# Placing the operands of 512-column products, and an earlier copy of x, in a four-layer float32 trunk

## The chip, the core and the metric

The kernel runs on one core of a Trainium2 chip. The metric is the time of one execution on the device in microseconds (us), the median of several. A profile is one further execution, recorded instruction by instruction. Engines: PE (TensorE: products), DVE (VectorE), ACT (ScalarE), POOL (GpSimd) and SP (SyncE); the last two mainly issue DMAs here.

## The reference

512 rows of 1,024 columns, all in float32, go through four layers. Each layer adds a mixer's output to x and then a gated FFN's; a root-mean-square norm precedes both, and one ends the trunk.

```python
for layer in range(DEPTH):            # 4
    h = rmsnorm(x, norm_mix[layer])
    mix = (s5_mixer, gla_mixer, diff_attn_mixer)[layer % 3](h, ...)
    x = x + mix
    h = rmsnorm(x, norm_ffn[layer])
    g, u = split(h @ w_gate_up, 2)    # 1024 x 5632
    x = x + (silu(g) * u) @ w_down    # 2816 x 1024
return rmsnorm(x, norm_final)
```

Layers 0 and 3 have the S5 mixer (a diagonal state space scan, a GELU and a gated product with `w_glu`, 1024 x 2048), layer 1 gated linear attention, layer 2 differential attention (eight heads, each of two softmaxes).

## The kernel before

**Products.** A float32 operand is kept as two float32r parts, a high part (ACT casts, L334) and a low part (DVE subtracts, L338). A product is three PE instructions: high x high, high x low, low x high (`mm3`, L351 to L353). The first operand of `matmul` after the output is held in the array in pieces of 128 columns; the second streams through it, 512 columns at a time. In `gemm_b` (down products, GLU, output products) the weights' parts `whl` stream and the activations are held: `act` in the FFNs, `zT` after S5, `oT` after the attentions, `hT` for the projections. In `gemm_a` (the first FFN's gate and up products, L351 to L353 with the tile name `any`) the weights are held and `hT` streams. The scores of differential attention (L1916) hold `qs` and stream `ks`.

**The fast FFN.** FFNs 1 to 3 use a Strassen-like scheme with seven products of quarters, 256 columns wide (L566). `seven_block` makes one block of 256 hidden columns: `one` to `seven` are the products, `*_out` take results out of PSUM, `gate1` and `four_out` apply SiLU, `add` sums weight quarters. The streamed sides are quarters of x and sums of them: "11" and "12" (tile `sides`) and "1", "2", "4", "3", "22" (tiles `side`). `left.total`, `high` and `low` form them. Weight quarters are loaded by SP; sums of two are formed by a second DMA on POOL that accumulates (L602, argument `plus`). The eleven blocks go in groups of 4, 4 and 3, each followed by a down product over 512-column halves.

**Order around the change.** Between the calls of `hand_all` and `hand` the order of every engine is that of the program text; elsewhere only PE's is (in the attentions), or a scheduler orders by priority and dependence. The string `plan` in `ffn` writes out the head of an FFN, blocks 0 ("a") and 1 ("b") interleaved. `ahead` stages weights of the first blocks while the mixer's last product still runs; at the second one it calls `total("3")`, two DVE subtractions (L199).

**The copy of x.** Layer 3's S5 wants the rows in another order. So the third FFN (`turn=True`) sends x to DRAM and back (`turn_x`, L804 and L806, each 2 MB, issued by POOL), and the row factors r with it. It is called at block 2, after that block's last accumulating DMA. POOL is in order: it waits at L806 until L804 has landed.

**Places in SBUF.** Tiles of a pool lie one behind the other, pools of a layer begin where the long-lived pools end. Adding up their sizes: the tiles of `hp` (hT, halves, sides) and `wp` (whl, wst) start at 192 modulo 256 bytes; the small pool (`self.sp`) has eight rooms of 32 bytes for each of its names and ends at 132,992, which is 128 modulo 256. So the layers' tiles (act, oT, side, slot, hl, qs) start at 128. zT is in a pool at the right end of SBUF, at 224.

**Heads of attention.** `prepare(j)` (L1885) splits a head's q and k into `hl` (one room), and eight small POOL DMAs rearrange it into `qs` and `ks`; `ks` lies in a weights' room (`wp`, name whl, five rooms).

**Norms with a power.** `normed` (L442) is used for the opening norm and the last one: Square on ACT (L450), an add on DVE (L437), a power on POOL (L439), then the scaling. `ms` holds the sums.

Of the kernel before, what the change touches and what calls it, by code (L numbers as in the profile page):

```python
# [11 lines left out]
F32 = mybir.dt.float32  # L12
# [4 lines left out]
ALU = mybir.AluOpType  # L17
# [128 lines left out]
class Sides(Left):  # L146
# [18 lines left out]
    def ahead(self, n):  # L165

        w = [self.tr.staged(self.quarter(0, 0, b), 4, 256) for b in range(len(self.heads), len(self.heads) + n)]
        self.heads += [self.tr.halves(y, 4, 256) for y in w]
        if len(self.heads) == 2:
            self.total("3")  # L170

    def open(self, pool, names):

# [89 lines left out]
class Trunk:  # L263
    def __init__(self, ctx, tc, ins, out):
        self.ctx, self.tc, self.nc = ctx, tc, tc.nc
        self.i = ins
        self.out = out
        self.rot = 0
# [12 lines left out]
        self.two_pi = float(np.nextafter(np.float32(TWO_PI), np.float32(0)))  # L281
        self.mhalf = self.cp.tile([P, 8], F32, name="mhalf")
        nc.vector.memset(self.mhalf[:], -0.5)
        self.ones = self.cp.tile([P, P], F32, name="ones")
        nc.gpsimd.memset(self.ones[:], 1.0)
        self.dq = nc.sync
        self.jobs = iter(())
        self.pend = []
        self.guard, self.lazy = None, False

    def hand_all(self):
        E = mybir.EngineType
# [149 lines left out]
    def normed(self, xt, g, out, pool, aside=False):  # L442

        nc = self.nc
        if pool is None:
            junk = self.wp.tile([P, D], F32, tag="wst", name="sq", bufs=3)
        else:
            junk = pool.tile([P, D], F32, tag="sq", name="sq", bufs=2)
        ms = self.sp.tile([P, 1], F32, tag="ms", name="ms")
        nc.scalar.activation(junk[:], xt, AF.Square, scale=1.0 / 32.0, accum_out=ms[:])  # L450
        r = self.rsqrt(ms[:], 1, 1e-6)
        if out is None:
            h = pool.tile([P, D], F32, tag="h", name="h", bufs=2)
            nc.vector.scalar_tensor_tensor(h[:], xt, r[:], g[:], op0=ALU.mult, op1=ALU.mult)
            return h
        if aside:
            nc.scalar.mul(junk[:], xt, r[:])
            gr = lambda y: y.rearrange("p (g c) -> p g c", c=16)
            nc.gpsimd.tensor_tensor(out, gr(junk[:]), gr(g[:]), op=ALU.mult)
# [45 lines left out]
    def ffn_plain(self, l, left, after=None, aside=None):  # L505
# [2 lines left out]
        wgu, wd = i["ffn_w_gate_up"][l], i["ffn_w_down"][l]  # L508
        nxt = None
        with self.tc.tile_pool(name=f"ffn{l}", bufs=1, reuse_waits="tile") as fp:  # L510
            self.jobs = aside(fp) if aside else iter(())
            first = True
            j0 = 0
# [57 lines left out]
    def seven_block(self, fp, slots, left, wgu, b, turn):  # L571
# [20 lines left out]
        def load(name, q, half, plus=None, room=None):  # L592
            if name in ("11", "3"):
                W[name] = self.staged(left.quarter(q, half, b), 4, 256)
            else:
                W[name] = slots.pop(0) if room is None else room
                if room is not None:
                    lent.add(name)
                nc.sync.dma_start(W[name][:], left.quarter(q, half, b))
            w = W[name]  # L600
            if plus:
                self.added = nc.gpsimd.dma_start(w[:], left.quarter(*plus, b), accum_op=ALU.add)  # L602

        def done(name):
            if name not in lent:
# [106 lines left out]
    def ffn(self, l, left, after=None, turn=False, aside=None):  # L712
# [5 lines left out]
        with self.tc.tile_pool(name=f"ffn{l}", bufs=1, reuse_waits="tile") as fp:  # L718

            room = lambda: fp.tile([P, 2, 4, 256], F32, tag="act", name="lent", bufs=4)  # L720
            left.open(fp, ("1", "2", "4", "3", "22") if l < 3 else ("1", "2"))
            if l == 3:
                lent = room()
            slots = [fp.tile([P, 4, 256], F32, name=f"slot{n}") for n in range(SLOTS)]
# [4 lines left out]
            blocks = [self.seven_block(fp, slots, left, wgu, b, turn) for b in range(FFN_HIDDEN // 256)]  # L729
            f = blocks[:2]  # L730
            if l == 3:
                left.open(fp, ("4", "3", "22"))
            for w, n, *room in (
                ("room21", 0), ("room1", 0, lent[:, 0]), ("room21", 1), ("room1", 1, lent[:, 1]), ("room22", 0),
# [1 line left out]
            ):  # L736
                f[n][w](*room)

            plan = """
                split21a one:a split21b square flush one:b total1 one_out:a finish high1 low1 total2 split1a high2 low2  # L740
                one_out:b two:a two:b split1b high3 two_out:a five:a add22a highSa two_out:b lowSa five_out:a five:b
                add22b highSb diag lowSb low3 split3a six:a spread five_out:b rows six:b six_out:a split3b seven:a
                six_out:b total4 split22a high4 low4 seven:b seven_out:a split22b three:a seven_out:b gate1:a gate1:b
                high22 low22 three:b add21a highFa add21b lowFa highFb lowFb four:a four:b three_out:a three_out:b
            """
            for step in plan.split():
                name, _, n = step.partition(":")
                if n:
# [5 lines left out]
                elif name in ("finish", "diag", "spread", "rows"):  # L754
                    getattr(left, name)()
                elif name == "square":
                    left.square(NT - 1, 1)
                elif name == "flush":
                    self.flush()
                else:  # L760
                    word = next(w for w in ("total", "high", "low") if name.startswith(w))
                    getattr(left, word)(name[len(word) :])
# [5 lines left out]
            for nb in (4, 4, 3):  # L768
                acts = []
                for n in range(b0, b0 + nb):  # L770
                    b = blocks[n]
                    if n > 1:
                        for w in ("direct", "room1", "room22", "room21", "summed"):
                            b[w]()
                    if turn and n == 2:

                        with self.tc.issue_after(self.added.ins):
                            r = self.turn_x(left.r)
                    if n > 1:
                        for step in ("one", "one_out", "five", "five_out"):  # L780
                            b[step]()
# [599 lines left out]
    def s5_first(self, ctx):  # L1381
        nc, i = self.nc, self.i
        xin = self.xp.tile([P, NT, D], F32, tag="x", name="xin")
        zpool = ctx.enter_context(self.tc.tile_pool(name="zT0", bufs=1, side="right"))
        zT = zpool.tile([P, 2, KT, SEQ], F32R, name="zT")
        with self.tc.tile_pool(name="s5_0", bufs=1) as p:
            scr, more = (self.hp.tile([P, 4096], F32, tag="hT", name=f"scr{z}") for z in range(2))
            oms = [more[:, 1024 * z : 1024 * z + 1024].rearrange("p (a b) -> p a b", a=2) for z in range(2)]
# [73 lines left out]
    def s5_second(self, l, ctx, left):  # L1462
        nc = self.nc
        zpool = ctx.enter_context(self.tc.tile_pool(name="zT1", bufs=1, side="right"))
        zT = zpool.tile([P, 2, KT, SEQ], F32R, name="zT")
        with self.tc.tile_pool(name="s5_1", bufs=1) as p:
            room = p.tile([P, 6, 512], F32, name="room2")
            parts = (("in", 0, 2, 2), ("cs", 2, 5, 3), ("out", 5, 8, 2))
# [26 lines left out]
    def s5_glu(self, L, zT, accs, after):  # L1495
# [5 lines left out]
        with self.tc.tile_pool(name=f"s5g_{L}", bufs=1) as p:  # L1501
            for d in range(2):
# [15 lines left out]
                        evac_b(t, accs[t])  # L1518
                else:
                    self.gemm_b(stat, wg, KT, D + d * 512, evac_b)  # L1520
                ahead = (lambda: nxt.ahead(2)) if L and d else None
                self.gemm_b(stat, wg, KT, d * 512, evac_a, tail=4 if d else 0, ahead=ahead)
        return nxt

# [1 line left out]
    def gla(self, l, left, after):  # L1526
# [3 lines left out]
        wo = i["gla_w_o"][0]  # L1530
        self.hand(mybir.EngineType.PE)
        with self.tc.tile_pool(name="gla", bufs=1) as p:
            big = lambda name, tag="g8", bufs=5: p.tile([P, 4, 512], F32, tag=tag, name=name, bufs=bufs)
            late = lambda name: big(name, "g8late", 3)
            oT = [p.tile([P, 2, 4, SEQ], F32R, name="oT0"), None]
# [195 lines left out]
            for d in range(2):  # L1731
                self.gemm_b(
                    so, wo, KT, d * 512, self.add_x(d, nxt), tail=4 if d else 0, between=() if d else late,
                    ahead=(lambda: nxt.ahead(2)) if d else None,
                )
        return nxt

# [52 lines left out]
    def diff(self, l, left, after):  # L1790
# [2 lines left out]
        w, wo = i["diff_w_qkv"][0], i["diff_w_o"][0]  # L1793
        self.hand(mybir.EngineType.PE)
        with self.tc.tile_pool(name="diff", bufs=1) as p:
            T = lambda tag, bufs=2: p.tile([P, 512], F32, tag=tag, name=tag, bufs=bufs)
            oT = [p.tile([P, 2, 4, SEQ], F32R, name="oT0"), None]
            qks = [p.tile([P, 2, 4, SEQ], F32, tag="qk", name="qk", bufs=2) for _ in range(2)]
# [86 lines left out]
            def prepare(j):  # L1885


                hl = p.tile([P, 2, 2, SEQ], F32R, tag="hl", name="hl")
                src = qks[j // 4][:, :, j % 4]
                nc.scalar.copy(hl[:, 0], src)  # L1890
                v.tensor_tensor(hl[:, 1], src, hl[:, 0].bitcast(F32), op=ALU.subtract)
# [64 lines left out]

            def normalised(j):
                st, o_s = kept.pop(j)
                q2 = self.sp.tile([P, NT], F32, tag="q2", name="q2")
                v.tensor_tensor(q2[:], st[:, 0], st[:, 0], op=ALU.mult)  # L1960
                v.scalar_tensor_tensor(q2[:], q2[:], 1e-5, st[:, 1], op0=ALU.mult, op1=ALU.add)
                rs = self.rsqrt(q2[:], NT, 0.0)
# [175 lines left out]
```

## Time and profile before

| | |
|---|---|
| median of 3 runs | 2391.58 us (2383.74, 2391.58, 2391.62) |
| profiled execution | 2382.31 us, its span 2380.6 us |
| granted PE clock | 0.982 of full speed, mean |
| ACT, DVE busy | 1073.0 us (45%), 1487.1 us (62%) |
| HBM read, written | 275.92 MB, 23.99 MB |

The span runs from the first to the last instruction. A row of the timeline has its start, its duration, the engine, the line, the operation, output and inputs, shapes, and in brackets the idle time before it with what ended it. The duration of a PE instruction is its latency; the next starts earlier, so the rate is the distance between starts. PEld is the loading of the held operand, which overlaps PE.

### The profile page before, as it was taken

To read this page: it belongs to the slowest core of one execution; us is meant where nothing else is said; L and a number is where in the kernel's file an instruction comes from. 1 tells how busy PE (TensorE), PEld (TensorE's weight loads), DVE (VectorE), ACT (ScalarE), POOL (GpSimd) and SP (SyncE) were. 2 spreads that over 40 slices of the span, in tenths; PEclk is the share of its full clock that TensorE was granted. 3 is DMA by queue.
4 is the path that set the end of the run, shared out by engine and by line. 5 is a ranking of instruction groups with operands and counts; after the bars stand their busy time and mean duration, and the time that the engine had idled before them with its cause. 6 is when DMAs were issued, how large, how long until landed. Compare 5 with 4: busy or idle time off the path is not lost. (4 is left out here: it accounts for less than half of the span.)

```text
span 2380.6 us, 35208 instructions
## 1 busy us (share of the span) xinstructions
PE 2269.0 (95%) x14055; PEld 1962.8 (82%) x14055; DVE 1487.1 (62%) x2311; ACT 1073.0 (45%) x1749; POOL 266.8 (11%) x335
## 2 busy tenths in 40 slices
PE   4799999999999999999999998989999899999997
PEld 3578888788877789898987887888989788999996
DVE  7774565555443459585753666875847874967674
ACT  4463445444352346252544665653635233634442
POOL 3330100111000011010001221110000000101000
PEclk9699999999999999999999999999999899999999
DMA  4123344544332258564345465694732645666521
GB/s 110 34 52 138 95 138 143 166 129 166 118 103 85 71 143 208 137 177 124 111 142 117 107 133 145 170 243 115 195 98 89 214 158 150 170 179 154 162 76 67
DMA packets 275502, 317.42 MB, mean 133 GB/s; under 512 B 45653, under 2 KB 214377, under 8 KB 274058
## 3 DMA queue, kind: packets, MB, share of 16 engines
q1 hardware_dynamic: 227210, 238.14, 31.9%
q0 software_dynamic: 48128, 77.02, 15.7%
q8 instruction: 111, 1.82, 0.3%
q14 instruction: 53, 0.43, 0.1%
HBM read 275.92 MB, written 23.99 MB: 126 GB/s over the span
## 5 line engine op out<-in xcount | busy, mean ns | idle before, releaser
L338 DVE TENSOR_TENSOR whl<-wst,whl 128x1024 fp32r<-128x1024 f32 x294 | 359.0, 1223 | 363.1 <-ACT whl L334 362.3
L334 ACT CAST whl<-wst 128x1024 fp32r<-128x1024 f32 x294 | 308.4, 1050 | 530.5 <-PE acc L353 354.8
L566 PE MATMUL a<-side,whl 128*128 128x256 f32 x2376 | 291.2, 279 | 14.2 <-ACT r L638 6.0
L566 PEld LDWEIGHTS a<-side,whl 128*128 128x128 f32 x2376 | 281.4, 190 | 16.2 <-ACT whl L334 6.9
L351 PE MATMUL acc<-whl,act 128*128 128x512 f32 x704 | 276.5, 393 | 0.7 <-DVE g L611 0.7
L353 PE MATMUL acc<-whl,act 128*128 128x512 f32 x704 | 276.9, 393 | 0.0
L352 PE MATMUL acc<-whl,act 128*128 128x512 f32 x704 | 275.6, 391 | 0.0
L566 PE MATMUL c<-side,whl 128*128 128x256 f32 x1584 | 192.4, 278 | 3.6 <-DVE whl L338 3.6
L566 PEld LDWEIGHTS c<-side,whl 128*128 128x128 f32 x1584 | 186.9, 189 | 4.0 <-DVE whl L338 4.0
L351 PEld LDWEIGHTS acc<-whl,act 128*128 128x128 f32 x704 | 132.2, 188 | 30.9 <-DVE g L611 1.9
L352 PEld LDWEIGHTS acc<-whl,act 128*128 128x128 f32 x704 | 132.2, 188 | 28.8
L353 PEld LDWEIGHTS acc<-whl,act 128*128 128x128 f32 x704 | 132.3, 188 | 27.9
L351 PE MATMUL any<-hT,whl 128*128 128x512 f32 x384 | 151.7, 395 | 0.0
L352 PE MATMUL any<-hT,whl 128*128 128x512 f32 x384 | 149.6, 390 | 0.0
L353 PE MATMUL any<-hT,whl 128*128 128x512 f32 x384 | 149.6, 389 | 0.0
L351 PE MATMUL acc<-whl,hT 128*128 128x512 f32 x352 | 143.8, 408 | 1.1 <-ACT whl L334 0.6
L352 PE MATMUL acc<-whl,hT 128*128 128x512 f32 x352 | 138.6, 394 | 1.0 <-DVE whl L338 1.0
L353 PE MATMUL acc<-whl,hT 128*128 128x512 f32 x352 | 139.0, 395 | 0.0
L338 DVE TENSOR_TENSOR whl<-halves,whl 128x1024 fp32r<-128x1024 f32 x72 | 87.7, 1222 | 32.5 <-ACT whl L334 32.5
L352 PE MATMUL acc<-whl,zT 128*128 128x512 f32 x256 | 103.9, 406 | 4.1 <-DVE whl L338 4.1
L334 ACT CAST whl<-halves 128x1024 fp32r<-128x1024 f32 x72 | 75.3, 1052 | 69.2 <-PE acc L353 26.7
L351 PE MATMUL acc<-whl,zT 128*128 128x512 f32 x256 | 102.8, 406 | 2.7 <-ACT zT L468 2.7
(438 smaller groups left out, 4185.1 us busy)
## 6 DMA issues: line engine op xcount, KB each, us to landing
wst<-in_ffn_w_gate_up_dram SPq DMA_DIRECT2D x110, 512.0 KB, 4.0
wst<-in_ffn_w_down_dram SPq DMA_DIRECT2D x88, 512.0 KB, 3.7
halves<-in_ffn_w_gate_up_dram SPq DMA_DIRECT2D x42, 512.0 KB, 5.9
slot<-in_ffn_w_gate_up_dram SPq DMA_DIRECT2D x39, 512.0 KB, 6.6
wst<-in_ffn_w_gate_up_dram POOLq DMA_DIRECT2D x33, 512.0 KB, 6.4
wst<-in_s_w_glu_dram SPq DMA_DIRECT2D x32, 512.0 KB, 3.6
spill<-opsp POOLq DMA_DIRECT2D x8, 2048.0 KB, 8.7
wst<-in_gla_w_in_dram SPq DMA_DIRECT2D x24, 512.0 KB, 3.6
```

The costliest lines, as they stand in the source:

```text
L334: self.nc.scalar.copy(hl[:, 0], w[:])
L338: self.nc.vector.tensor_tensor(hl[:, 1], w[:], hl[:, 0].bitcast(F32), op=ALU.subtract)
L351: mm(out, lh, rh, start=first, stop=False)
L352: mm(out, lh, rl, start=False, stop=False)
L353: mm(out, ll, rh, start=False, stop=last)
L566: mm(o, hl[:, x, k, c], side[:, y, k], start=first and not (j or k or n), stop=k == 3 and n == 2, skip_group_check=True,)
```

## The change

Four things, in one diff.

1. `edge` allocates an unused tile of n bytes per partition in a pool. It stands at the start of the plain FFN's pool, of both attentions' pools (64 bytes), after the sides of the fast FFNs (64), again before the late sides of the last FFN (192), and beside zT (32). To make room, `ms` has two rooms in place of eight and `q2` six. No instruction goes with an edge.
2. In the third FFN the copy of x is a step `turn` in the head's plan, behind `five:b`; POOL reaches it right behind the power of `finish`. That FFN has a plan of its own: `total3` is a step of it, and `seven_out:b`, `gate1:a` and `gate1:b` come behind the casts of weights 22 and of the sums that `four` needs. The other FFNs keep their plan, and `total("3")` is called where the mixers stage weights.
3. At the end of differential attention the first two row blocks of the last product are taken out one step earlier, and the second `ahead` comes after the last row block has been taken out.
4. The parts `hl` of head 1 lie in a weights' room.

```diff
@@ Sides.ahead
         self.heads += [self.tr.halves(y, 4, 256) for y in w]
-        if len(self.heads) == 2:
-            self.total("3")
@@ Trunk
+    def edge(self, pool, n):
+        self.edges += 1
+        pool.tile([P, n // 4], F32, name=f"edge{self.edges}", bufs=1)
@@ normed
-        ms = self.sp.tile([P, 1], F32, tag="ms", name="ms")
+        ms = self.sp.tile([P, 1], F32, tag="ms", name="ms", bufs=2)
@@ ffn_plain
+            self.edge(fp, 64)
@@ seven_block, load
-                self.added = nc.gpsimd.dma_start(w[:], left.quarter(*plus, b), accum_op=ALU.add)
+                nc.gpsimd.dma_start(w[:], left.quarter(*plus, b), accum_op=ALU.add)
@@ ffn
             left.open(fp, ("1", "2", "4", "3", "22") if l < 3 else ("1", "2"))
+            self.edge(fp, 64)
...
             if l == 3:
+                self.edge(fp, 192)
                 left.open(fp, ("4", "3", "22"))
...
+            if l == 2:
+                plan = """
+                    split21a one:a split21b square flush one:b total3 total1 one_out:a finish high1 low1 total2 split1a
+                    high2 low2 one_out:b two:a two:b split1b high3 two_out:a five:a add22a highSa two_out:b lowSa
+                    five_out:a five:b turn add22b highSb diag lowSb low3 split3a six:a spread five_out:b rows six:b
+                    six_out:a split3b seven:a six_out:b total4 split22a high4 low4 seven:b seven_out:a split22b
+                    high22 low22 three:a add21a highFa add21b lowFa highFb three:b lowFb seven_out:b gate1:a four:a gate1:b
+                    four:b three_out:a three_out:b
+                """
+            else:
                 plan = """
...
                     six_out:b total4 split22a high4 low4 seven:b seven_out:a split22b three:a seven_out:b gate1:a gate1:b
                     high22 low22 three:b add21a highFa add21b lowFa highFb lowFb four:a four:b three_out:a three_out:b
                 """
...
+                elif name == "turn":
+                    r = self.turn_x(left.r) if turn else r
...
-                    if turn and n == 2:
-                        with self.tc.issue_after(self.added.ins):
-                            r = self.turn_x(left.r)
@@ s5_first, s5_second
         zT = zpool.tile([P, 2, KT, SEQ], F32R, name="zT")
+        self.edge(zpool, 32)
@@ s5_glu, gla
-                ahead = (lambda: nxt.ahead(2)) if L and d else None
+                ahead = (lambda: (nxt.ahead(2), nxt.total("3"))) if L and d else None
@@ gla, diff
+            self.edge(p, 64)
@@ diff, prepare
-                hl = p.tile([P, 2, 2, SEQ], F32R, tag="hl", name="hl")
+                room, bufs, tag = (self.wp, 5, "whl") if j == 1 else (p, 1, "hl")
+                hl = room.tile([P, 2, 2, SEQ], F32R, tag=tag, name="hl", bufs=bufs)
@@ diff, normalised
-                q2 = self.sp.tile([P, NT], F32, tag="q2", name="q2")
+                q2 = self.sp.tile([P, NT], F32, tag="q2", name="q2", bufs=6)
@@ diff, the end
             between = {
-                2: {1: (one,), 3: (one, lambda: evac(0, banks[0])), 5: (one, lambda: evac(1, banks[1])), 7: (one,)},
-                3: {1: (one,), 3: (one, lambda: nxt[0].ahead(1)), 5: (one,)},
+                2: {1: (one, lambda: evac(0, banks[0])), 3: (lambda: evac(1, banks[1]), one), 5: (one,), 7: (one,)},
+                3: {1: (one,), 3: (one,), 5: (one,)},
             }
...
                 evac(t, banks[t])
-                if t == 2:
-                    nxt[0].ahead(1)
+                nxt[0].ahead(1)
```

More of the change, by code (lines that the diff above doesn't have):

```diff
@@ L267, in __init__ @@
         self.out = out
-        self.rot = 0
+        self.rot = self.edges = 0
         nc = self.nc
@@ L737, in ffn @@
                 f[n][w](*room)
[L739 to L745, printed above, removed]
+            if l == 2:
[8 more added lines that the diff above has]
+            else:
+                plan = """
+                    split21a one:a split21b square flush one:b total1 one_out:a finish high1 low1 total2 split1a high2 low2
+                    one_out:b two:a two:b split1b high3 two_out:a five:a add22a highSa two_out:b lowSa five_out:a five:b
+                    add22b highSb diag lowSb low3 split3a six:a spread five_out:b rows six:b six_out:a split3b seven:a
+                    six_out:b total4 split22a high4 low4 seven:b seven_out:a split22b three:a seven_out:b gate1:a gate1:b
+                    high22 low22 three:b add21a highFa add21b lowFa highFb lowFb four:a four:b three_out:a three_out:b
+                """
             for step in plan.split():
@@ L1465, in s5_second @@
         zT = zpool.tile([P, 2, KT, SEQ], F32R, name="zT")
+        self.edge(zpool, 32)
         with self.tc.tile_pool(name="s5_1", bufs=1) as p:
@@ L1733, in gla @@
                     so, wo, KT, d * 512, self.add_x(d, nxt), tail=4 if d else 0, between=() if d else late,
-                    ahead=(lambda: nxt.ahead(2)) if d else None,
+                    ahead=(lambda: (nxt.ahead(2), nxt.total("3"))) if d else None,
                 )
@@ L1795, in diff @@
         with self.tc.tile_pool(name="diff", bufs=1) as p:
+            self.edge(p, 64)
             T = lambda tag, bufs=2: p.tile([P, 512], F32, tag=tag, name=tag, bufs=bufs)
```

## Prediction

> **What bounds the kernel now.** I read the page first, then the timeline of TensorE (PE), then the waits of the third FFN.
>
> ```profile
> span 2380.6 us, 35208 instructions
> PE 2269.0 (95%) x14055; PEld 1962.8 (82%) x14055; DVE 1487.1 (62%) x2311; ACT 1073.0 (45%) x1749; POOL 266.8 (11%) x335
> ```
>
> PE is busy for 95% of the span, so time can only come out of two places: the distance between one product's start and the next one's, and the few holes. The group view's mean (about 390 ns) is a product's latency; products overlap, so I take start to start from unbroken stretches of the PE timeline. Below are the first and the last row of five stretches, and three rows of merged 256-column products.
>
> ```profile
> 504.11 0.40 PE L352 MATMUL any<-hT,whl 128*128 128x512 f32 x1
> ...
> 525.48 0.39 PE L353 MATMUL any<-hT,whl 128*128 128x512 f32 x1
> ...
> 859.08 0.40 PE L352 MATMUL acc<-whl,oT 128*128 128x512 f32 x1
> ...
> 869.61 0.39 PE L353 MATMUL acc<-whl,oT 128*128 128x512 f32 x1
> ...
> 882.86 5.92 PE L566 MATMUL d<-sides,whl 128*128 128x256 f32 x48
> 888.62 5.62 PE L566 MATMUL c<-side,whl 128*128 128x256 f32 x48
> 894.08 2.89 PE L566 MATMUL a<-side,whl 128*128 128x256 f32 x24
> ...
> 1083.19 0.39 PE L351 MATMUL acc<-whl,act 128*128 128x512 f32 x1
> ...
> 1126.91 0.39 PE L353 MATMUL acc<-whl,act 128*128 128x512 f32 x1
> ...
> 1985.40 0.39 PE L352 MATMUL acc<-whl,zT 128*128 128x512 f32 x1
> ...
> 2018.53 0.39 PE L353 MATMUL acc<-whl,zT 128*128 128x512 f32 x1
> ```
>
> The stretches hold 95, 47, 192 and 143 products of 512 columns: hT 21.37/94 = 227.3 ns, oT 10.53/46 = 228.9, act 43.72/191 = 228.9, zT 33.13/142 = 233.3. The first name streams, the second is held. What differs between these four is where the operand beside the weights lies. Adding up the tiles of the pools, whl and hT start at 192 modulo 256 bytes, act and oT at 128, zT at 224. Equal places go with the smallest distance, 64 bytes apart costs 1.6 ns, 32 bytes apart 6.0 ns. The 256-column products do not follow this: sides (192, like whl) take 5.76/48 = 120.0 ns, side (128) 5.46/48 = 113.8.
>
> The holes: the third FFN's first four blocks run from 1503.02 to 1600.44, 97.4 us; the same 672 products of the second FFN run from 876.60 to 960.98, 84.4 us. Thirteen microseconds are lost there.
>
> ```profile
> 876.60 3.12 PE L566 MATMUL a<-sides,whl 128*128 128x256 f32 x24
> ...
> 924.12 2.77 PE L566 MATMUL c<-side,whl 128*128 128x256 f32 x22 [0.84 <-DVE whl L338]
> ...
> 960.98 0.39 PE L351 MATMUL acc<-whl,act 128*128 128x512 f32 x1
> ```
> ```profile
> 1503.02 3.02 PE L566 MATMUL a<-sides,whl 128*128 128x256 f32 x24
> ...
> 1507.72 0.63 PE L108 MATMUL tp<-ident,hh 128*128 128x128 f32 x4 [1.69 <-ACT sq L99]
> ...
> 1541.86 0.50 PE L566 MATMUL a<-side,whl 128*128 128x256 f32 x2 [1.96 <-ACT whl L334]
> ...
> 1543.12 5.50 PE L566 MATMUL a<-side,whl 128*128 128x256 f32 x46 [0.76 <-DVE whl L338]
> ...
> 1554.51 4.39 PE L566 MATMUL c<-side,whl 128*128 128x256 f32 x22 [2.79 <-DVE whl L338]
> ...
> 1575.61 2.90 PE L566 MATMUL c<-side,whl 128*128 128x256 f32 x24
> ...
> 1584.54 5.02 PE L566 MATMUL a<-side,whl 128*128 128x256 f32 x24 [6.04 <-ACT r L638]
> ...
> 1600.44 0.39 PE L351 MATMUL acc<-whl,act 128*128 128x512 f32 x1
> ```
>
> The largest hole, 6.04 us before 1584.54, waits for ACT's copy L638. That copy sits on ACT behind a cast that waited for a weight tile, and that tile's accumulating DMA was issued by POOL at 1571.35, after the round trip of x.
>
> ```profile
> 1518.73 1.33 POOL L602 DMA_DIRECT2D halves<-in_ffn_w_gate_up_dram  x1 [6.29 <-DMA halves<-in_ffn_w_gate_up_dram]
> ...
> 1533.68 1.30 POOL L804 DMA_DIRECT2D xturn<-vall  x1
> ...
> 1571.35 1.29 POOL L602 DMA_DIRECT2D wst<-in_ffn_w_gate_up_dram  x1 [9.24 <-DMA slot<-in_ffn_w_gate_up_dram]
> ```
> ```profile
> 1580.64 1.04 ACT L334 CAST whl<-wst 128x1024 fp32r<-128x1024 f32 x1 [7.09 <-DMA wst<-in_ffn_w_gate_up_dram]
> ```
> ```profile
> xturn<-vall POOLq DMA_DIRECT2D x1, 2048.0 KB, 22.0
> x<-xturn POOLq DMA_DIRECT2D x1, 2048.0 KB, 10.5
> ```
> ```profile
> 1508.00:1532.00 24.00, 24.00 (x208) 23.93 (x207) 21.84 (x27) 15.34 (x21) 2.35 (x2) 1.00 0.59 140
> 1532.00:1572.00 40.00, 34.49 (x280) 33.80 (x279) 36.74 (x45) 24.61 (x32) 7.22 (x8) 0.96 1.08 292
> 1582.00:1588.90 6.90, 4.36 (x20) 4.36 (x21) 6.37 (x7) 4.20 (x7) 0.00 (x0) 0.51 0.43 134
> ```
>
> In the windows view (length, busy times of PE, PEld, DVE, ACT, POOL, then PEclk, DMA share, GB/s) the DMA engines are full from 1532 to 1572 (share 1.08), while the two copies run, and only 0.59 busy in the 24 us before. The hole also costs clock: 0.51 granted from 1582 to 1588.9, so the 24 products from 1584.54 take 5.02 us where the 24 before them took 2.90: 2.1 us more.
>
> **The change, part by part.**
>
> *Places.* The small pool loses six ms rooms and two q2 rooms of 32 bytes, 256 in all, so every layer pool still starts at 128; the edges of 64 bytes push act, oT, qs and hl to 192, an edge of 32 bytes below the right end pulls zT from 224 to 192, and the sides keep 128 (in the last FFN by the further 192). So all 512-column products get the pair that hT has. Counts:
>
> ```profile
> L351 PE MATMUL acc<-whl,act 128*128 128x512 f32 x704 | 276.5, 393 | 0.7 <-DVE g L611 0.7
> ...
> L351 PE MATMUL acc<-whl,zT 128*128 128x512 f32 x256 | 102.8, 406 | 2.7 <-ACT zT L468 2.7
> ...
> L351 PE MATMUL acc<-whl,oT 128*128 128x512 f32 x128 | 53.4, 417 | 2.4 <-ACT oT L468 2.4
> ```
>
> Each is one of three lines. act: 2112 x 1.6 ns = 3.4 us, all on PE's path. zT: 768, of which 192 run inside the two S5 pipes, where PE waits for others; 576 x 6.0 = 3.5 us. oT: 384 x 1.6 = 0.6 us. The scores (ks, qs) I leave at nothing: they sit between waits. Sum 7.5 us. No row shows an operand moved by itself, so the low end is 0; the high end counts the pipes and 128 score products at zT's 6.0 ns too, 1.9 us more, 9.4. I take the sum, since four stretches order by distance alone. The Trainium skill, "TensorE: Matmul & The Clock Gate", Part 2, says that LDWEIGHTS and the streamed operand read SBUF through two independent ports, and that loading the next weights takes no bandwidth from the running product. By that rule places are indifferent, this term is 0 and the whole sum 9.4 us; the trace does not agree as it stands (227.3 against 233.3 ns).
>
> *Early copy of x.* xturn follows the rsqrt on POOL instead of the accumulate of block 2. POOL is in order and stands until each copy lands, so the accumulates of blocks 2 and 3 queue behind it. With 10.5 us per copy (the row under less load) from about 1513, POOL is free near 1535; block 2's first accumulate moves there from 1518.73, and PE asks for its product only near 1551.7 (2.79 us before 1554.51). Gone: 6.04 + 2.1 = 8.1 us. If the copies collide with the loads instead, the hole comes back: low end 0.
>
> *Order of the head.* Gates go behind the casts that four needs, which uncovers 1.96 + 0.76 = 2.7 us. DVE is busy 21.84 of 24 us here and the gates must still be done before block 2's bank is free, so I take 1.5. total3, 1.29 us of DVE, leaves the tail of attention, where it stands before the last x; the 1.69 us hole at 1507.72 closes, but the same 1.29 us come back in the head: 0.4. The wait of 2.79 us at 1554.51 (0.84 in the second FFN) comes from DVE's order and stays. Ends of these two together: 0 to 4.4; 1.9 taken. Second head weights cast after the last x: a product's third part needs them, covered by the 3 us of the first head.
>
> ```profile
> 1504.97 1.29 DVE L199 TENSOR_TENSOR s<-halves 128x512 f32<-128x512 f32 x2
> ```
>
> *Two ms rooms.* The opening norm's fourth Square must now wait for the second power on POOL.
>
> ```profile
> 21.72 1.06 ACT L450 ACTIVATE sq<-xin 128x1024 f32<-128x1024 f32 x1 [0.91 <-POOL scr L459]
> ...
> 29.11 1.15 ACT L457 ACTIVATE sq<-xin,rs 128x1024 f32<-128x1024 f32 x1 [2.52 <-POOL rs L439]
> ```
>
> It moves from 21.72 to about 29.1, beside L457, which feeds POOL: 0 if it goes behind, 1.1 if ahead, and up to 3 if it holds the casts queued behind it on ACT. PE is nearly idle there, so this is on the path; I take a loss of 0.6.
>
> *A head's parts in a weights' room.* ACT's wait of 2.16 us for the single hl room goes; it had no PE wait behind it, so 0. It holds one of five weight rooms for some 10 us: from +0.5 to -2 (a late weight costs about what the head's waits above do). q2 with six rooms, one used per four steps: nothing.
>
> ```profile
> 1290.57 1.05 ACT L1890 CAST hl<-qk 128x1024 fp32r<-128x1024 f32 x1 [2.16 <-DMA ks<-hl]
> ```
>
> Sum: 7.5 + 8.1 + 1.9 - 0.6 = 16.9 us (9.4 of it without the places). The profiled execution took 2382.3 us (span 2380.6), so 2365.4 in its kind. The runs shown lie at 2383.7, 2391.6 and 2391.6: with the profiled one two at each of two places, 8 to 9 us apart. I cannot tell where the next median falls and start from the middle, 2387.3: 2370.4 us. Against the median 2391.6, 0.5% (12 us, about what a measurement here can tell from no change) is 2379.6.
>
> **The rivals.**
>
> *Places do nothing* (the zT and act distances have another cause, or a tile lands elsewhere): only 9.4 us are left, 2378.0, or 2382.2 from the median's place. For it: the 256-column rows, where the equal place is the slower. Against: the stretches order by distance.
>
> *The hole moves.* The copies delay block 2's accumulate past 1551, and PE and clock lose the 8.1 us again in the head: 2378.5. For it: 22.0 us for one copy under load. Against: share 0.59 in the stretch it moves to.
>
> *Slower: the equal place is the bad one.* Place: every product of whl with act, oT and zT. By the 256-column rows it costs 6.2 ns per 256 streamed columns, 12.4 per 512; 2112 + 576 + 384 = 3072 products x 12.4 = 38 us, against 9.4 gained: 2387.3 + 28.7 = 2416. It decides from 3.1 ns per product on. For it: 120.0 against 113.8. Against: hT and whl, both at 192, have the smallest distance in 512.
>
> *Everything opens*: all 13.0 us of the FFN and 9.4 of the places: 2364.
>
> **How the numbers follow.** Forecast 0.64; everything opens 0.09; places do nothing 0.10; hole moves 0.13; slower 0.04. The range, 2359 to 2382, takes the forecast from the faster place of the runs (2365.4, less up to 6 for the high ends) to the two middle rivals with their unfavourable starts. Faster by over 0.5%: 0.64 + 0.09, and a third of the two middle rivals, less 0.02 for the forecast's edge: 0.79. Within 0.5%: 0.16. Slower: 0.05.
>
> **What would show it.** Right: zT and act stretches at 227 to 228 ns; xturn issued near 1513 and no PE wait of several microseconds before the third FFN's first down product; that stage at 84 to 89 us. Wrong: act or zT unchanged or near 240 ns; a PE wait on a cast of block 2 between 1540 and 1560 with the clock at 0.5; POOL's accumulates after 1545; PE's first S5 product later than now.

## The result and the profile after

After the change the median is 2367.14 us (2365.13 to 2369.29, four runs), beside 2387.66 us for the kernel before (2383.05 to 2391.62, four runs): ratio 0.9915, 95% interval 0.9889 to 0.9941. It is faster, by 0.9%. The profiled execution took 2365.13 us against 2382.31, 17.2 us less; the prediction's sum was 16.9. One of the four runs of old_gates below was slow throughout (2555.34 us, at a granted clock of 0.843) and is left out of its figures.

First the page of the kernel after: the busy times of the engines. PE executes the same 14,055 instructions and is busy 14 us less.

```profile
span 2363.4 us, 35206 instructions
...
PE 2254.8 (95%) x14055; PEld 1956.9 (83%) x14055; DVE 1486.4 (63%) x2311; ACT 1074.9 (45%) x1749; POOL 267.3 (11%) x335
```

Next the timeline of PE, first and last row of the same three stretches of 512-column products that the prediction measured (47 with oT, 192 with act, 143 with zT). Columns: start, latency, engine, line, operation.

```profile
858.93 0.40 PE L355 MATMUL acc<-whl,oT 128*128 128x512 f32 x1
...
869.39 0.39 PE L356 MATMUL acc<-whl,oT 128*128 128x512 f32 x1
...
1081.81 0.39 PE L354 MATMUL acc<-whl,act 128*128 128x512 f32 x1
...
1125.15 0.39 PE L356 MATMUL acc<-whl,act 128*128 128x512 f32 x1
...
1970.69 0.40 PE L355 MATMUL acc<-whl,zT 128*128 128x512 f32 x1
...
2002.92 0.39 PE L356 MATMUL acc<-whl,zT 128*128 128x512 f32 x1
```

Start to start: oT 10.46/46 = 227.4 ns (228.9 before), act 43.34/191 = 226.9 (228.9), zT 32.23/142 = 227.0 (233.3). All three now run as hT did.

The third FFN's first four blocks, in the same view:

```profile
1501.34 3.02 PE L570 MATMUL a<-sides,whl 128*128 128x256 f32 x24
...
1520.47 2.86 PE L570 MATMUL a<-side,whl 128*128 128x256 f32 x22 [0.76 <-DVE whl L341]
...
1550.68 4.39 PE L570 MATMUL c<-side,whl 128*128 128x256 f32 x22 [4.30 <-DVE whl L341]
...
1575.10 3.00 PE L570 MATMUL a<-side,whl 128*128 128x256 f32 x24 [0.40 <-ACT r L642]
...
1588.98 0.39 PE L354 MATMUL acc<-whl,act 128*128 128x512 f32 x1
```

The stage takes 87.6 us for 97.4. Of the five waits before (1.69, 1.96, 0.76, 2.79, 6.04 us) the first three are gone and the last is 0.40; the 2.79 us wait has grown to 4.30. The 0.76 us at 1520.47 is a new wait, at a place where before had none. POOL's own timeline shows the copy of x where the plan puts it:

```profile
1510.32 0.83 POOL L818 DMA_DIRECT2D xturn<-vall  x1
1520.97 1.28 POOL L606 DMA_DIRECT2D halves<-in_ffn_w_gate_up_dram  x1 [9.82 <-issue]
1521.74 1.09 POOL L820 DMA_DIRECT2D x<-xturn  x1
...
1540.35 1.33 POOL L606 DMA_DIRECT2D wst<-in_ffn_w_gate_up_dram  x1 [0.28 <-issue]
```

Where the 17.2 us came from, by the start of each stage's first product in the two timelines (us): opening up to the first GLU +3.8; first S5's products -1.7; first FFN -0.6; gated attention -1.8; second FFN -1.9; differential attention +0.4; third FFN with the scan behind it -11.4 (first four blocks -9.8); second S5's products -2.7; fourth FFN -1.5; the end 0.0.

The +3.8 is no fixed price of the change. One row of the windows view of after (length, PE busy with the number of its instructions, granted clock, DMA share, GB/s) has half the clock in a stretch that before ran at full clock:

```profile
141.00:151.20 10.20, 10.20 (x37) 0.50 0.01 2
```

Of the twelve kernels below, with the same products at that place, two show this window (half_sides, half_late) and ten do not; one of the ten, places_only, has half the clock for 3.4 us at 139.9. The Trainium skill, "TensorE: Matmul & The Clock Gate", Part 1, says that the clock follows PE's activity over free-running windows of about 3.4 us, so the same kernel can fall on either side; the lengths agree (10.2 here, 3.4 and 6.8 elsewhere). What makes it fall there is not settled. Clock explains a gain too: before has a granted clock of 0.51 from 721.8 to 725.3, in the gated attention's projections, where after has 1.00, and the same 96 products take 23.2 us there and 21.7 in after. So 1.5 of the gated attention's 1.8 us is not shown to be the change's.

### The profile page after: what moved, and what is told of

Same layout as the page of the kernel before. It is cut to its first block, busy times and chain, and to the rows that moved or that the text cites. A ratio compares the mean times of both kernels' runs of the same rounds, so it can differ in the third digit from the quotient of the medians.

```text
span 2363.4 us, 35206 instructions
## 1 busy us (share of the span) xinstructions
PE 2254.8 (95%) x14055; PEld 1956.9 (83%) x14055; DVE 1486.4 (63%) x2311; ACT 1074.9 (45%) x1749; POOL 267.3 (11%) x335
```

## The experiments

The rivals that the runs are to tell apart: places do nothing; the order did the copy's work; VectorE sets the point behind the wait, so that the order gives nothing. The kernels were measured in three rounds, each beside before anew (medians of before 2384.74, 2386.79 and 2383.93 us), so their ratios can be compared across rounds and their medians less well.

**places_only**: before, with the edges, two rooms for `ms` and six for `q2`, and nothing else.

```diff
@@ normed
-        ms = self.sp.tile([P, 1], F32, tag="ms", name="ms")
+        ms = self.sp.tile([P, 1], F32, tag="ms", name="ms", bufs=2)
@@ ffn_plain
+            self.edge(fp, 64)
...
```

> The kernel before with the edges and the smaller small pool alone; the copy of x and the plan stay as they were. If the place of the held rows sets the rate: zT, act and oT stretches at 227 to 228 ns, the third FFN's first four blocks still at about 97 us, and 7 to 8 us less than the kernel before (ratio 0.997). If the place does nothing and the rate came down with the new order of work: stretches at 229 and 233 ns, ratio 1.000.

Median 2378.34 us against 2384.74, ratio 0.9977 (0.9967 to 0.9988): 5.5 us, between 2.9 and 7.9. act, oT and zT run at 227 to 228.7 ns. The third FFN's first blocks take 97.6 us (97.4 before) and its waits stand about as before, the largest at 4.3 us where it was 6.0 (engine, output, line, releaser; us in total, times, longest):

```profile
PE a L572 <- ACT r L644: 4.3, 1, 4.3
PE a L572 <- ACT whl L339: 2.4, 2, 2.0
PE tp L108 <- ACT sq L99: 1.7, 1, 1.7
```

**head_only**: after, with `edge` doing nothing.

```diff
     def edge(self, pool, n):
-        self.edges += 1
-        pool.tile([P, n // 4], F32, name=f"edge{self.edges}", bufs=1)
+        pass
```

> The changed kernel with every edge left out, so that act and oT are held at 128 and zT at 224 again; all of the new order stays. If places and copy are two separate gains: stretches back at 229 and 233 ns, the third FFN's first four blocks at 87 to 88 us as in the changed kernel, 9 to 10 us less than the kernel before (ratio 0.996). If the copy gains only together with the places: the blocks at 90 us or more.

Median 2378.42 us, ratio 0.9964 (0.9951 to 0.9978): 8.6 us. act is back at 229.0 ns, zT at 233.2; the third FFN's first blocks take 88.9 us. The ratios of the two halves multiply to 0.9941, 14 us, the upper end of the whole change's interval; what is missing to its 20 us by the medians lies inside the intervals.

**sweep**: after, with the held operand at other places, a different one in each stage.

```diff
@@ ffn_plain
-            self.edge(fp, 64)
+            self.edge(fp, 96)
@@ ffn
-            self.edge(fp, 64)
+            self.edge(fp, {1: 32, 2: 128, 3: 192}[l])
...
@@ s5_second
-        self.edge(zpool, 32)
+        self.edge(zpool, 96)
@@ gla
-            self.edge(p, 64)
+            self.edge(p, 160)
```

> The changed kernel with other edges: act held at 224, 160, 0 and 64 modulo 256 in the four FFNs, oT of the linear attention at 32, the second zT at 128; whl streams at 192 throughout. If what counts is the distance from the streamed place, with a sign for neither side: 233 ns at 224 and 160 (32 away), 229 at 0 and 128 (64 away), and something else at 64 (128 away) and 32 (96 away). If only a shift by an odd multiple of 32 hurts: 233 at 224, 160 and 32, 227 to 229 at 0, 64 and 128. If zT's strided writing was what made it slow: zT at 128 stays at 233.

In the timeline of PE, the stretches with act of the second (place 160), third (0) and fourth FFN (64), with 182, 182 and 192 products:

```profile
979.42 0.39 PE L355 MATMUL acc<-whl,act 128*128 128x512 f32 x1
...
1021.65 0.39 PE L356 MATMUL acc<-whl,act 128*128 128x512 f32 x1
...
1609.44 0.39 PE L355 MATMUL acc<-whl,act 128*128 128x512 f32 x1
...
1651.67 0.40 PE L356 MATMUL acc<-whl,act 128*128 128x512 f32 x1
...
2116.86 0.39 PE L354 MATMUL acc<-whl,act 128*128 128x512 f32 x1
...
2161.24 0.40 PE L356 MATMUL acc<-whl,act 128*128 128x512 f32 x1
```

That is 42.23/181 = 233.3, 42.23/181 = 233.3 and 44.38/191 = 232.4 ns. With the other stages, read in the same way, for 512 columns and the streamed weights at 192:

| held operand at, modulo 256 | 192 | 128 | 64 | 0 | 160 | 224 | 32 |
|---|---|---|---|---|---|---|---|
| ns per product | 226.9 | 229.0 | 232.4 | 233.3 | 233.3 | 233.3 | 234.3 |
| tile | act, zT | zT | act | act | act | act | oT |

The same tile takes several rates in one run, by its place alone. Equal is best; 64 below the weights costs 2.1 ns and 64 above (0) 6.4, so the direction counts beside the distance. None of the rules named ahead of the run fits: by distance alone 0 would cost what 128 does, by odd multiples of 32 both 0 and 64 would be as fast as 128, and zT at 128 would have stayed slow if the way it is written had been the cause. The weights lay at 192 in every kernel, so the runs do not tell the distance between the two operands from the place of the moved one alone, and why a place costs time stays open.

The run took 2390.4 us, 23 more than after, and 27 without the half clock that after has at 141 us. The rates explain some 15: 1,584 products of act x 6.4, 528 x 5.5, and oT and zT 2. Another 11 are in the second FFN's head, whose first blocks take 95.4 us for 84.4, with a new wait of 5.1 us and half the clock for 6.8 us from 896.6 on. SP's row for the first weight slot, here of after and then of sweep, shows why:

```profile
841.03 0.46 SPq L603 DMA_DIRECT2D slot<-in_ffn_w_gate_up_dram  x1
```
```profile
880.48 0.37 SPq L603 DMA_DIRECT2D slot<-in_ffn_w_gate_up_dram  x1
```

Adding up the tiles, with unequal edges in the attention's pool and the FFN's the first weight slot of the FFN (bytes 173,728 to 177,824) overlaps the tail of the attention's held operand oT (up to 173,856); in after oT ends and slot 0 begins at 173,760. The slot's load is issued 0.5 us behind the start of the last output product (880.02), and SP is in order: the loads behind it come 39 us late.

**side192**: after, with the tiles `side` of the fast FFNs at 192 instead of 128.

```diff
+            self.edge(fp, 64)
             left.open(fp, ("1", "2", "4", "3", "22") if l < 3 else ("1", "2"))
-            self.edge(fp, 64)
```

> The changed kernel with the edge of the fast FFNs ahead of the sides, so that the streamed side tiles lie at 192 like whl, as sides does; act stays at 192. If the equal place is the slow one for 256 columns: side products at 120 ns in place of 113.8, 3960 x 6.2 = 24 us more than the changed kernel. If sides is slow for another reason (it comes first, with fresh weights): side stays at 114 ns and the time does not move.

One run: 2385.45 us, span 2383.7, 20.3 us above after's, 24 without the half clock that after has at 141 us. The runs of 24 products in PE's timeline:

```profile
1006.06 3.04 PE L570 MATMUL a<-sides,whl 128*128 128x256 f32 x24
1008.93 3.04 PE L570 MATMUL c<-side,whl 128*128 128x256 f32 x24
1011.81 3.04 PE L570 MATMUL a<-side,whl 128*128 128x256 f32 x24
```

2.88/24 = 120.0 ns with side, as with sides, where after has 2.72/24 = 113.3. So for 256 columns the equal place is the bad one. (Here the streamed operand was moved and the weights were held; with 512 columns the held one was moved and the weights streamed.) The rule of the places holds for one width; a guess from one to the other would be wrong either way.

**turn_late**: after, with the copy of x behind the last accumulating DMA of block 2 again.

```diff
-                    five_out:a five:b turn add22b ...
+                    five_out:a five:b add22b ...
+                        if turn and n == 2:
+                            with self.tc.issue_after(self.added.ins):
+                                r = self.turn_x(left.r)
```

> After, with x copied through DRAM behind the last added piece of block 2 again (as before the change); the plan of steps, the gates and the places stay. If the early copy is worth the 8.1 us of the prediction (a TensorE hole of about 6 us ahead of the third FFN's fourth block, and the half clock behind it), the third FFN's first four blocks take about 95.5 us where after takes 87.6, and the whole is 0.3% above after, 2375 us. If the new order of steps made most of the gain, the stage stays under 91 us and the whole under 2371.

Median 2374.07 us, ratio 0.9946 (0.9928 to 0.9965). The first blocks take 94.5 us, 6.8 more than after. Timelines of PE and then POOL:

```profile
1551.42 4.33 PE L570 MATMUL c<-side,whl 128*128 128x256 f32 x22 [4.30 <-DVE whl L341]
1580.35 4.85 PE L570 MATMUL a<-side,whl 128*128 128x256 f32 x21 [4.99 <-ACT r L642]
```
```profile
1532.42 1.30 POOL L821 DMA_DIRECT2D xturn<-vall  x1
...
1554.05 0.57 POOL L823 DMA_DIRECT2D x<-xturn  x1 [12.07 <-DMA xturn<-vall]
...
1567.32 1.32 POOL L606 DMA_DIRECT2D wst<-in_ffn_w_gate_up_dram  x1 [11.46 <-DVE halves L663]
```

The wait before `six` of block 3 is back with 4.99 us (0.40 in after), and so is the half clock behind it: 21 products with a busy time of 4.85 us. Only the copy was moved, so the wait is the copy's.

**old_gates**: after, with the old order of steps in the third FFN; `turn` and `total3` stay where they are. In effect:

```diff
-                    high22 low22 three:a add21a highFa add21b lowFa highFb three:b lowFb seven_out:b gate1:a four:a gate1:b
+                    three:a seven_out:b gate1:a gate1:b high22 low22 three:b add21a highFa add21b lowFa highFb lowFb four:a
```

> After, with the third FFN's steps in the old order (gate products ahead of the casts of 22, four behind all casts), the early copy and total3 kept. The prediction gave the order 1.5 us: the stage would be 89 us. Rival, from the trace of after: VectorE is busy without a pause up to the cast that TensorE waits for at 1550.7 us, and the same cast came at 1553.2 before; if VectorE sets that point, what the order saves ahead of it is given back there, and the old order costs nothing: a wait of about 2.2 us comes back ahead of the first four product, the 4.6 us wait behind it shrinks by as much, and the stage stays at 87 to 88 us. A third outcome, over 90 us, would say that the order moves VectorE's work forward too, and that the prediction priced it too low.

Median 2368.52 us of three runs, ratio 0.9923 (0.9902 to 0.9943). The first blocks take 89.2 us, 1.6 more than after:

```profile
1540.16 0.50 PE L570 MATMUL a<-side,whl 128*128 128x256 f32 x2 [1.96 <-ACT whl L337]
1541.42 7.22 PE L570 MATMUL a<-side,whl 128*128 128x256 f32 x46 [0.76 <-DVE whl L341]
1553.35 2.79 PE L570 MATMUL c<-side,whl 128*128 128x256 f32 x22 [1.60 <-DVE whl L341]
```

1.96 + 0.76 us come back ahead of `four`, with a granted clock of 0.57 from 1541 to 1545, and the wait behind shrinks from 4.30 to 1.60. Both theories see part of it: most of what the order saves is given back at one cast, and 1.6 us stays. DVE's timeline in after shows who holds that cast: it stands behind four_out's subtractions and DVE has no pause.

```profile
1548.30 0.69 DVE L697 TENSOR_TENSOR r<-g,r 128x512 f32<-128x512 f32 x1
1548.90 0.60 DVE L708 TENSOR_TENSOR act<-r,act 128x256 fp32r<-128x256 f32 x1
1549.41 1.22 DVE L341 TENSOR_TENSOR whl<-halves,whl 128x1024 fp32r<-128x1024 f32 x1
```

Before, the same cast started at 1553.22: DVE is 3.8 us earlier, PE is 5.3 us earlier at the same product, and the difference is the longer wait.

**sides128, half_sides, half_late**: the sides 11 and 12, which the change leaves at 192, also 64 bytes from the weights: both, 12 alone, or 11 alone. To make room, four kinds of small tiles get four rooms in place of eight.

```diff
-        two = self.tr.hp.tile([P, 2, 2, 4, 256], F32R, tag="hT", name="sides")
-        self.place = {"11": two[:, 0], "12": two[:, 1]}
+        two = self.tr.hp.tile([P, 4096 + 64], F32R, tag="hT", name="sides")
+        self.place = {
+            n: two[:, at : at + 2048].rearrange("p (y k n) -> p y k n", y=2, k=4)
+            for n, at in (("11", 0), ("12", 2096))     # half_sides; both: 48, 2096; half_late: 48, 2112
+        }
```

> After, with the streamed sides 11 and 12 at place 128 modulo 256 too, 64 bytes from the held pieces of the weights at 192 (a view 192 bytes into a room that is 256 bytes longer; four kinds of small tiles get 4 rooms for 8). Where the place sets the rate, the 1584 products of 256 columns that take 119.4 ns on the mean go to 113.7, as the other sides have it: 1584 x 5.6 ns = 8.9 us, 2358 us for the whole, ratio to before 0.988. If the sides 11 and 12 are slow for another reason (they are the first product of each group), they stay at 119 to 120 and the whole at 2367.

Median 2371.67 us, ratio 0.9944 (0.9923 to 0.9966): no gain over after. In the second FFN's first blocks nearly all products ran at 113 to 114 ns, as expected; in the second group of blocks not one did:

```profile
1003.17 2.99 PE L571 MATMUL a<-sides,whl 128*128 128x256 f32 x24
1005.99 2.99 PE L571 MATMUL c<-side,whl 128*128 128x256 f32 x24
1008.82 2.99 PE L571 MATMUL a<-side,whl 128*128 128x256 f32 x24
```

2.83/24 = 117.8 ns, for `side` too, which nothing had moved. So there are two steady rates at this distance, and the gain was lost to the slow one. The kernel best, sides128 with the new order in all three fast FFNs, fell into it as well:

> The kernel of sides128, and the second and fourth FFN take the third one's new order of steps too. These two have waits of 2.2 and 1.0 us ahead of their first four product and a wait of 0.9 and 0.5 us behind it, no 4.6 us one: with the order, up to 3.2 us go in each, 2 x 2.5 us less what comes back behind: 2353 us, ratio to before 0.986. If VectorE sets the point behind them there as well, nothing goes and it stays with sides128.

Median 2371.39 us, ratio 0.9937 (0.9921 to 0.9953), with 117.8 ns in the later groups. That gave a new theory, tried by the next two kernels.

> After, with side 12 alone moved to place 128; side 11, the first of a block's seven products, stays at 192. With both moved, every product of the later blocks took 117.8 ns, without a change from the first product behind the 512-column stage to the last of four blocks, while the first blocks ran at 113.4. Theory: at 64 bytes apart there are two steady rates, 113.3 and 117.8; a stage of 512 columns ahead leaves the slow one, and a run of products at the equal place (120.0) leaves the fast one, as after shows it (121, 121, 116, 114, 114, 113 at the start of side 1). Then here six of seven products take 113.3 in every block and one 120: mean 114.3 against after's 115.2, 5544 x 0.95 = 5 us, 2362 us. Rival: too many products at 113.3 in a row bring the slow rate whatever came first; then the six stand at 117.8, mean 118, and the whole is over 2375 us.

> The mirror: side 11 at 128 and side 12, the fourth of the seven products of a later block, at 192. By the theory a stage's first three products (72 instructions behind the 512-column stage) take 117.8 ns, the fourth 120, and all others up to the stage's end 113.3, with 120 for the fourth of each block. By the rival the rate goes back to 117.8 some products behind each fourth, or stays there.

half_late, timeline of PE behind the down product:

```profile
1006.99 2.99 PE L573 MATMUL c<-side,whl 128*128 128x256 f32 x24
1009.81 2.99 PE L573 MATMUL a<-side,whl 128*128 128x256 f32 x24
1012.64 3.04 PE L573 MATMUL d<-sides,whl 128*128 128x256 f32 x24
1015.51 2.90 PE L573 MATMUL a<-side,whl 128*128 128x256 f32 x24
1018.25 2.88 PE L573 MATMUL c<-side,whl 128*128 128x256 f32 x24
1020.97 2.88 PE L573 MATMUL a<-side,whl 128*128 128x256 f32 x24
```

2.83 us per 24 (117.8 ns) until the run at the equal place (2.87, 119.6), then 2.74 and 2.72 (113.3), and so on to the end of the stage. In half_sides, where the equal run comes first, the other six runs of the later groups have 113 to 114 ns throughout, and 672 products take 76.7 us for 77.3 in after. In the later groups of both kernels the theory holds: the rate that a stretch falls into is left by what ran ahead of it, and stays. Two readings of other traces limit it. In before and head_only, where the down product has act 64 bytes apart, the first run at the equal place left the slow rate in nine of twelve later groups (117.7 ns for the next two runs), and only the second such run ended it. And behind a wait either rate comes: the same wait in the second FFN's head, 0.72 us from start to start, turned 117.8 into 113.3 ns in sides128 and was followed by 117.8 in half_sides. What decides there is open. half_sides has median 2361.9 us, ratio 0.9912 (0.9896 to 0.9928); against after's 0.9915 that is no difference that shows, though every later group is shorter by 0.5 to 0.6 us. half_late took 2362.11 in its one run.

**order_all, best2**: the new order in the second and fourth FFN too, alone and on half_sides.

```diff
-            if l == 2:
+            if True:
...
-                    getattr(left, word)(name[len(word) :])
+                    if name != "total3" or l == 2:
+                        getattr(left, word)(name[len(word) :])
```

> After, with the new order of steps in the second and fourth FFN too, the places as in after. The order alone gave 1.6 us in the third FFN (stage 89.1 with the old order, 87.5 with the new). In the kernel with both sides moved it took 2.1 us off the second FFN's first blocks and 0.8 off the fourth's, and gave 1.4 back and 0.9 more in the products behind. So 1 to 3 us: 2365 us, ratio to before 0.990; the rival is no difference that shows.

> half_sides and order_all together: 5 and 2 us below after, 2360 us, ratio to before 0.989 or lower. If half_sides falls to the slow rate, over 2373.

order_all: 2362.55 us, ratio 0.9926 (0.9903 to 0.9948), not told apart from after. best2: 2358.09 us, ratio 0.9902 (0.9885 to 0.9919), the lowest median of all, and in its waits the second FFN's head has one of 2.4 us where after has 2.0, 0.8 and 0.6 (engine, output, line, releaser; us, times, longest):

```profile
PE c L573 <- DVE whl L344: 2.4, 1, 2.4
```

Its first blocks take 82.0 us in the second FFN (84.4 in after) and 82.5 in the fourth (84.8), the down products behind them up to 1.6 more. The two were never run beside each other. Their medians differ by 9 us, but those of before differ by 4 between the two rounds; by the ratios best2 is 3 us ahead, and the intervals overlap. Faster than before is shown, faster than after is not.

## Why the prediction came out right, step by step

- **Places, 7.5 us.** The mechanism is shown: sweep moves nothing but places and the rates follow. By the rates the term is 2112 x 2.0 + 576 x 6.3 + 384 x 1.5 = 8.4 us; measured alone, 5.5 (2.9 to 7.9), so the sum by rates is a little above what the run bears out. The step that act, 64 apart, costs 1.6 ns was a little low (2.0), because hT's stretch, the yardstick, was itself a little slow. Scores at nothing was right: 231.5 ns before and 231.8 after, although they are at equal places now. So the place does not set the rate of every 512-column product; what sets theirs was not tried. The Trainium skill's rule of two independent read ports ("TensorE: Matmul & The Clock Gate", Part 2), by which the term would be 0, does not agree with 226.9 to 233.3 ns for act by its place alone. The prediction's order by distance alone failed in sweep (0 and 128 are equally far), but the change uses only equal places, so nothing hung on it.
- **Early copy, 8.1 us.** turn_late puts it at 6.8. Laid over each other product by product from the stage's start, before and after say 7.7: after is 2.1 us ahead just before the old 6.04 us wait and 9.8 at the end. xturn left at 1510.3 (forecast 1513) and the two copies took 8.7 and 11.5 us (forecast 10.5 each). Two details differed: block 2's first accumulate slipped in between the copies, at 1520.97, and POOL was free at 1540.35, not 1535, since it also stands 15.9 us for the row factors. Neither reached PE.
- **Order, 1.5 of 1.9 us.** old_gates gives 1.6. But the step "the wait of 2.79 us comes from DVE's order and stays" failed: it is 4.30 now. The waits of 2.7 us did go whole, and DVE took a good part back at the next cast. The prediction's discount for a busy DVE was of the right size, but it was placed at block 2's bank; that the total came out right is in part luck.
- **total3 and the last row blocks, 0.4 us.** The wait of 1.69 us at the transposes is gone in every kernel with the change's head, and after is 1.8 us ahead there. Most of it comes back, as forecast, in part as the new wait of 0.76 us at 1520.47: from 1523.98 on, before `four`, after is ahead by 0.4 us, the number forecast. This is a reading of two timelines; no run changes `total3` alone. The runs' own shares (copy 6.8, order 1.6) leave 1.4 of the 9.8 us for it; the 1.0 between may be their interplay, since the wait that comes back in turn_late is 4.99 us and not 6.04.
- **Two rooms, -0.6 us.** The fourth Square went from 21.72 to 30.87, behind the scaling, the case priced at 0. The first GLU's products begin at 148.59 before and at 147.1 to 149.7 in the ten kernels that have two rooms and lack the 10.2 us of half clock: no loss that shows against that scatter.
- **A head's parts in a weights' room, 0.** From the first projection to the last output product of differential attention it takes 281.3 us before, 281.7 after, and 281.6 in places_only, which lacks this edit: nothing that shows, as forecast, against 279.2 to 282.6 in the others.
- **The rivals.** Places do nothing and the hole moves are out. The slower one had a true half: the equal place is the slow one, at 256 columns, and side192 shows its price; at 512 it is the fast one. "Everything opens" did not come, because of the 4.30 us.
- **The start of the sum.** The middle of before's two places, 2387.3, against a median of 2387.66 in the comparison. The medians fell by 20.5 us, 3.6 more than the sum. That the two profiles differ by 17.2, so near to 16.9, is luck in part: half clock in places that the change does not aim at cost after 3.8 us and before 1.5. (By its own terms "Everything opens" gives 2364.9 us and not 2364.)

## What to carry to other kernels

Compare rates of the same kind of product across stages, start to start, before asking what waits: three per cent of a product's time hid here in where a tile happens to lie, and a rule of that kind has to be measured for each width, since in these kernels 256 and 512 columns want opposite things. When a tile is moved, look also at what it lies over: unequal edges put one slot on a tile still in use, and that cost 11 us. A wait removed ahead of a busy engine comes back at the next point which that engine sets, so read its timeline up to there before counting the gain.

## What the runs showed of the hardware

- The rate of back-to-back products with weights at 192 modulo 256 bytes depends on where the other operand starts: 226.9 to 234.3 ns for 512 columns, 113.3 to 120.0 for 256, with equal places at opposite ends. The scores of attention, 231.5 and 231.8 ns, did not follow it.
- 256-column products 64 bytes apart have two steady rates, 113.3 and 117.8 ns. One lasted unchanged over the 672 products of a group. A first run of 24 at the equal place left the fast one in every later group of eight kernels, but in only three of twelve in before and head_only, where act lay 64 bytes apart; behind a wait either rate came.
- A wait of some 4 us on PE was followed by half the clock for 3.4 us (4.39 us for 22 products that take 2.5 at full clock), and a stretch with short waits only, near 141 us, had half the clock for 10.2 us in three kernels, for 3.4 in one and not at all in nine.
